# The cosine table of a rotary embedding loaded in two transfers, rows 0 to 15 and rows 16 to 127

## The chip, the core and the metric

The kernel runs on one core of a Trainium2 chip. The core has a vector engine (DVE), a scalar engine (ACT), GpSimd (POOL), a sync engine (SP) and a tensor engine (PE), which this kernel leaves idle, and sixteen DMA engines that move data between the device's memory (HBM) and the on-chip memory, whose 128 partitions are the rows of a tile. The metric is the device time of one execution in microseconds, the median of three runs.

## The reference

Rotary position embedding on x of shape (batch 8, sequence 2048, 16 heads, 64 features), float32, with tables cos and sin of shape (2048, 32):

```python
x1 = x[..., :head_dim // 2]
x2 = x[..., head_dim // 2:]
cos = cos[None, :, None, :]
sin = sin[None, :, None, :]
out1 = x1 * cos - x2 * sin
out2 = x1 * sin + x2 * cos
return np.concatenate([out1, out2], axis=-1).astype(np.float32)
```

## The kernel before

One tile is one batch element. The 2048 positions are laid over 128 partitions, J = 16 consecutive positions to a partition, so a tile is 128 x 16384 numbers: 64 KB of float32 per partition in HBM, 32 KB of float16 on the chip. The eight tiles are loaded by DMAs that POOL issues (`load`, L54) and that turn float32 into float16 on the way; DVE rotates a tile in three passes (`rotate`: the product with sin into v, L75; the product with cos in place, L81; the sum, L83); DMAs from POOL store the tile back, float16 to float32 (`store`, L62). Five buffers hold tiles, so load b + 5 waits until store b has landed.

Three loads go through SP's own DMA queue, which doesn't convert: sin (L42), the first four positions of each partition of tile 0 as float32 (`head`, JA = 4, L43, 16 KB per partition), and cos (L47, 2 KB per partition), in this order. POOL's load of tile 0 therefore brings only positions 4 to 15 (48 KB per partition in HBM).

ACT turns these into float16: it writes sin twice into sin_h, once negated (L94, L95), narrows head's first position (JF = 1, `narrow_head(0, JF)`, L89), narrows cos into cos_h (L97), then head's other three positions (L89 again). DVE rotates the first position of tile 0 by itself (128 x 1024), and POOL stores it at once as `first` (L108, `store_rows`).

Order around the start. Each engine runs its own instructions in order. The order on POOL is fixed by hand for the start (`ring`): load 0, load 1, the first store, load 2, load 3, load 4; then the stores and loads of the main loop. The first store waits for DVE's L83 on the first position, which waits for L81, which needs cos_h. The order of the other engines' instructions comes from a scheduler that starts from the order of the program and may move instructions that don't depend on each other.

The end: the last tile goes out in three parts, positions 0 to 8 (L136), 9 to 13 (L138) and, as float32 through ACT's copy `tail` (L147) and SP's queue (L148), positions 14 and 15, which wait until the first part has landed.

Of the kernel before, what the change touches and what calls it, by code (L numbers as in the profile page):

```python
# [1 line left out]

# [4 lines left out]


@with_exitstack  # L10
def kernel(
    ctx: ExitStack,
    tc: tile.TileContext,
    x: bass.AP,
    cos: bass.AP,
    sin: bass.AP,
    out: bass.AP,
):
    nc = tc.nc
    f16 = mybir.dt.float16  # L20
    f32 = mybir.dt.float32

    B, S, H, D = x.shape
    Dh = D // 2
    P = nc.NUM_PARTITIONS
    J = S // P
    NBUF = 5

    const_pool = ctx.enter_context(tc.tile_pool(name="rope_const", bufs=1))
    io_pool = ctx.enter_context(tc.tile_pool(name="rope_io", bufs=NBUF))  # L30
    tmp_pool = ctx.enter_context(tc.tile_pool(name="rope_tmp", bufs=1))

    JA = 4
    JE = 2
    JF = 1
    head = io_pool.tile([P, JA, H, D], f32, tag="xt")
    x0 = x[0].rearrange("(p j) h d -> p j (h d)", j=J)
    sin_f = const_pool.tile([P, J, Dh], f32)
    cos_f = const_pool.tile([P, J, Dh], f32)
    cos_h = const_pool.tile([P, J, Dh], f16)  # L40
    sin_h = const_pool.tile([P, J, D], f16)
    nc.sync.dma_start(out=sin_f, in_=sin.rearrange("(p j) d -> p j d", j=J))  # L42
    nc.sync.dma_start(  # L43
        out=head.rearrange("p j h d -> p (j h d)"),
        in_=x0[:, 0:JA, :].rearrange("p j f -> p (j f)"),
    )
    nc.sync.dma_start(out=cos_f, in_=cos.rearrange("(p j) d -> p j d", j=J))  # L47

    loads = []

    def load(b):
        xt = io_pool.tile([P, J, H, D], f16, tag="xt")
        j0 = JA if b == 0 else 0
        dma = nc.gpsimd.dma_start(  # L54
            out=xt[:, j0:J, :, :].rearrange("p j h d -> p (j h d)"),
            in_=x[b].rearrange("(p j) h d -> p j (h d)", j=J)[:, j0:J, :].rearrange("p j f -> p (j f)"),
        )
        loads.append(dma)
        return xt

    def store(b, xt, j0=0):
        return nc.gpsimd.dma_start(  # L62
            out=out[b].rearrange("(p j) h d -> p j (h d)", j=J)[:, j0:J, :].rearrange("p j f -> p (j f)"),
            in_=xt[:, j0:J, :, :].rearrange("p j h d -> p (j h d)"),
        )

    def rotate(xt, j0, j1):
        v = tmp_pool.tile([P, J, H, D], f16)
        n = j1 - j0
        js = slice(j0, j1)  # L70
        shape = [P, n, H, 2, Dh]
        sin_b = sin_h[:, js, :].rearrange("p j (e d) -> p j e d", e=2).unsqueeze(2).to_broadcast(shape)
        cos_b = cos_h[:, js, :].unsqueeze(2).to_broadcast([P, n, 2 * H, Dh])
        xe = xt[:, js, :, :].rearrange("p j h (e d) -> p j h e d", e=2)
        nc.vector.tensor_mul(  # L75
            out=v[:, js, :, :].rearrange("p j h (e d) -> p j h e d", e=2),
            in0=xe[:, :, :, ::-1, :],
            in1=sin_b,
        )
        xw = xt[:, js, :, :].rearrange("p j h (e d) -> p j (h e) d", d=Dh)  # L80
        nc.vector.tensor_mul(out=xw, in0=xw, in1=cos_b)  # L81
        xa = xt[:, js, :, :].rearrange("p j h d -> p (j h d)")
        nc.vector.tensor_add(out=xa, in0=xa, in1=v[:, js, :, :].rearrange("p j h d -> p (j h d)"))  # L83


    tiles = [load(0)]
    tiles.append(load(1))
    def narrow_head(j0, j1):
        nc.scalar.copy(  # L89
            out=tiles[0][:, j0:j1, :, :].rearrange("p j h d -> p (j h d)"),  # L90
            in_=head[:, j0:j1, :, :].rearrange("p j h d -> p (j h d)"),
        )

    nc.scalar.copy(out=sin_h[:, :, Dh:D], in_=sin_f)  # L94
    nc.scalar.mul(out=sin_h[:, :, 0:Dh], in_=sin_f, mul=-1.0)  # L95
    narrow_head(0, JF)
    nc.scalar.copy(out=cos_h, in_=cos_f)  # L97
    narrow_head(JF, JA)
    rotate(tiles[0], 0, JF)
    def part(b, j0, j1):  # L100
        return (
            out[b].rearrange("(p j) h d -> p j (h d)", j=J)[:, j0:j1, :].rearrange("p j f -> p (j f)"),
            tiles[b][:, j0:j1, :, :].rearrange("p j h d -> p (j h d)"),
        )

    def store_rows(b, j0, j1):
        dst, src = part(b, j0, j1)
        return nc.gpsimd.dma_start(out=dst, in_=src)  # L108

    first = store_rows(0, 0, JF)  # L110
    ring = [loads[0], loads[1], first]
    for b in range(2, NBUF):
        tiles.append(load(b))
        ring.append(loads[b])
    for a, b in zip(ring[1:], ring[:-1]):
        tc.add_manual_dep(
            a.ins,
            b.ins.name,
            mybir.DependencyInfo(mybir.DependencyClass.NoSync, mybir.DependencyReason.DATA),
            reason="order of the ring",  # L120
        )
    for b in range(B):
        rotate(tiles[b], JF if b == 0 else 0, J)
        if b < B - 1:
            st = store(b, tiles[b], JF if b == 0 else 0)
            if b == 0:
                tc.add_manual_dep(
                    st.ins,
                    first.ins.name,
                    mybir.DependencyInfo(mybir.DependencyClass.NoSync, mybir.DependencyReason.DATA),  # L130
                    reason="order of the ring",
                )
        if b + NBUF < B:
            tiles.append(load(b + NBUF))
    dst, src = part(B - 1, 0, 9)
    gate = nc.gpsimd.dma_start(out=dst, in_=src)  # L136
    dst, src = part(B - 1, 9, J - JE)
    rest = nc.gpsimd.dma_start(out=dst, in_=src)  # L138
    tc.add_manual_dep(
        rest.ins,  # L140
        gate.ins.name,
        mybir.DependencyInfo(mybir.DependencyClass.NoSync, mybir.DependencyReason.DATA),
        reason="order of the ring",
    )
    dst, src = part(B - 1, J - JE, J)
    tail = io_pool.tile([P, JE, H, D], f32, tag="xt")
    nc.scalar.copy(out=tail.rearrange("p j h d -> p (j h d)"), in_=src)  # L147
    end = nc.sync.dma_start(out=dst, in_=tail.rearrange("p j h d -> p (j h d)"))  # L148
    tc.add_manual_dep(
        end.ins,  # L150
        gate.ins.name,
        mybir.DependencyInfo(mybir.DependencyClass.Sync, mybir.DependencyReason.DATA),
        reason="the last rows go out behind this part",
    )


# [1 line left out]
_INS = ['x', 'cos', 'sin']  # L158
_OUTS = [((8, 2048, 16, 64), 'float32')]


# [23 lines left out]
```

## Time and profile before

| | |
|---|---|
| median of three runs | 316.67 us (316.46 to 317.0) |
| profiled execution, first to last instruction (span) | 314.8 us; no other time is listed for it |
| DVE busy | 209.1 us, 66% of the span |
| DMA moved | HBM read 67.63 MB, written 67.11 MB, 428 GB/s over the span |
| sin: issue to landing | 2.8 us, 256 KB |
| head: issue to landing | 16.4 us, 2048 KB |
| cos: issue to landing | 34.1 us, 256 KB |
| load 0: issue to landing | 22.0 us, 3072 KB on the chip |
| first store: issue to landing | 6.4 us, 512 KB on the chip |

Two views matter most. The chain of waits follows the last instruction back to what released it; the timeline lists instructions with start, length, engine and line, and in brackets how long the engine sat idle before and what ended that. "q0" are the packets of DMAs that POOL issued, "q1" those that SP issued. Beside these views the trace keeps a record of each DMA packet, with start, length, size and queue: one packet per row of a transfer, and for each DMA engine a 4-byte completion packet that counts up the semaphore. Landing times are those of the last of sixteen completions.

### The profile page before, as it was taken

The numbers are of one execution on the slowest core, as the hardware profiler recorded it, in microseconds if no ns is written. First come the engines' busy times: TensorE is split into PE (matmuls) and PEld (weight loads), VectorE is DVE, ScalarE is ACT, GpSimd is POOL, SyncE is SP. The second block draws the span as 40 slices with busy tenths as digits, with TensorE's granted clock in tenths as the row PEclk, the third lists the DMA queues.
The fourth block names the chain that finished last, engine by engine and source line by source line (L and its number), as shares of the span: only waits on it lengthen the run. The fifth ranks groups of instructions, "written<-read, shape, count | busy, mean of one in ns | idle before, by whom it ended". The sixth has DMA issues, their size and how long they took to land.

```text
span 314.8 us, 126 instructions
## 1 busy us (share of the span) xinstructions
DVE 209.1 (66%) x27; ACT 8.6 (3%) x7; POOL 9.9 (3%) x22
## 2 busy tenths in 40 slices
DVE  0000299999999999999999999999009993000000
ACT  3010400000000000000000000000000002000000
POOL 1000110000000000010000000200000001000000
DMA  8999999999999899999999999999999999999998
GB/s 262 287 233 212 204 267 200 200 266 200 200 200 325 375 500 400 400 333 266 200 200 208 391 400 400 458 475 266 200 266 466 400 400 516 416 400 400 433 425 341
DMA packets 3168, 102.24 MB, mean 325 GB/s; under 512 B 352, under 2 KB 352, under 8 KB 736
## 3 DMA queue, kind: packets, MB, share of 16 engines
q0 software_dynamic: 2592, 98.57, 97.4%
q1 hardware_dynamic: 576, 3.67, 3.0%
HBM read 67.63 MB, written 67.11 MB: 428 GB/s over the span
## 4 chain that ended last, share of the span: by engine, by line
DMA 39%; DVE 24%; issue 18%; ACT 2%; POOL 0%; SPq 0%; POOLq 0%; DVEq 0%
DMA out_dram<-xt 16%; DMA xt<-in_x_dram 12%; DMA cos_f<-in_cos_dram 11%; DVE xt L83 8%; DVE xt L81 8%; DVE v L75 8%; ACT xt L89 1%; ACT tail L147 1%; POOL out_dram L62 0%; ACT cos_h L97 0%; POOL xt L54 0%; SPq L43 0%; SPq L42 0%; POOLq L54 0%; DVEq L75 0%
## 5 line engine op out<-in xcount | busy, mean ns | idle before, releaser
L75 DVE TENSOR_TENSOR v<-xt,sin_h 128x16384 f16<-128x16384 f16 (+2 forms) x9 | 69.7, 7744 | 35.9 <-ACT xt L89 19.8
L81 DVE TENSOR_TENSOR xt<-xt,cos_h 128x16384 f16<-128x16384 f16 (+2 forms) x9 | 69.7, 7744 | 17.4 <-ACT cos_h L97 17.1
L83 DVE TENSOR_TENSOR xt<-xt,v 128x16384 f16<-128x16384 f16 (+2 forms) x9 | 69.7, 7744 | 0.3
L147 ACT CAST tail<-xt 128x2048 f32<-128x2048 f16 x1 | 1.9, 1898 | 223.7 <-DVE xt L83 223.7
L54 POOL DMA_DIRECT2D xt<-in_x_dram x8 | 4.4, 555 | 105.4 <-DMA out_dram<-xt 104.6
L62 POOL DMA_DIRECT2D out_dram<-xt x7 | 3.7, 535 | 71.4 <-DVE xt L83 71.4
L89 ACT CAST xt<-head 128x1024 f16<-128x1024 f32 (+1 forms) x2 | 3.8, 1896 | 12.9 <-DMA head<-in_x_dram 12.9
L136 POOL DMA_DIRECT2D out_dram<-xt x1 | 0.5, 531 | 41.5 <-DVE xt L83 41.5
L108 POOL DMA_DIRECT2D out_dram<-xt x1 | 0.5, 536 | 35.7 <-DVE xt L83 35.7
L94 ACT ACT_TABLE_LOAD x1 | 1.3, 1283 | 0.7 <-PEq L169 0.7
L97 ACT CAST cos_h<-cos_f 128x512 f16<-128x512 f32 x1 | 0.6, 617 | 17.2 <-DMA cos_f<-in_cos_dram 17.2
L94 ACT CAST sin_h<-sin_f 128x512 f16<-128x512 f32 x1 | 0.6, 617 | 1.5 <-DMA sin_f<-in_sin_dram 1.5
L95 ACT ACTIVATE sin_h<-sin_f 128x512 f16<-128x512 f32 x1 | 0.6, 624 | 0.0
L138 POOL DMA_DIRECT2D out_dram<-xt x1 | 0.5, 531 | 0.0
L169 POOL MEMSET const-float32-0.0<- 128x1 f32 x1 | 0.1, 98 | 0.2 <-issue 0.2
L169 POOL MEMSET const-bfloat16-1.0<- 128x1 bf16 x1 | 0.1, 102 | 0.0
L169 POOL MEMSET const-float32-1.0<- 128x1 f32 x1 | 0.1, 98 | 0.0
L169 POOL MEMSET const-uint8-127<- 128x1 uint8 x1 | 0.1, 98 | 0.0
## 6 DMA issues: line engine op xcount, KB each, us to landing
xt<-in_x_dram POOLq DMA_DIRECT2D x7, 4096.0 KB, 38.3
out_dram<-xt POOLq DMA_DIRECT2D x1, 7680.0 KB, 56.7
out_dram<-xt POOLq DMA_DIRECT2D x1, 4608.0 KB, 42.4
xt<-in_x_dram POOLq DMA_DIRECT2D x1, 3072.0 KB, 22.0
out_dram<-xt POOLq DMA_DIRECT2D x1, 2560.0 KB, 47.9
head<-in_x_dram SPq DMA_DIRECT2D x1, 2048.0 KB, 16.4
out_dram<-tail SPq DMA_DIRECT2D x1, 1024.0 KB, 8.4
out_dram<-xt POOLq DMA_DIRECT2D x1, 512.0 KB, 6.4
```

Of the source, the lines that this page charges most:

```text
L54: dma = nc.gpsimd.dma_start(out=xt[:, j0:J, :, :].rearrange("p j h d -> p (j h d)"), in_=x[b].rearrange("(p j) h d -> p j (h d)", j=J)[:, ...
L62: return nc.gpsimd.dma_start(out=out[b].rearrange("(p j) h d -> p j (h d)", j=J)[:, j0:J, :].rearrange("p j f -> p (j f)"), in_=xt[:, j0:J ...
L75: nc.vector.tensor_mul(out=v[:, js, :, :].rearrange("p j h (e d) -> p j h e d", e=2), in0=xe[:, :, :, ::-1, :], in1=sin_b,)
L81: nc.vector.tensor_mul(out=xw, in0=xw, in1=cos_b)
L83: nc.vector.tensor_add(out=xa, in0=xa, in1=v[:, js, :, :].rearrange("p j h d -> p (j h d)"))
L89: nc.scalar.copy(out=tiles[0][:, j0:j1, :, :].rearrange("p j h d -> p (j h d)"), in_=head[:, j0:j1, :, :].rearrange("p j h d -> p (j h d)"),)
L94: nc.scalar.copy(out=sin_h[:, :, Dh:D], in_=sin_f)
L95: nc.scalar.mul(out=sin_h[:, :, 0:Dh], in_=sin_f, mul=-1.0)
L97: nc.scalar.copy(out=cos_h, in_=cos_f)
L108: return nc.gpsimd.dma_start(out=dst, in_=src)
L136: gate = nc.gpsimd.dma_start(out=dst, in_=src)
L147: nc.scalar.copy(out=tail.rearrange("p j h d -> p (j h d)"), in_=src)
```

## The change

The DMA that SP issues for cos is replaced by two, in the same place of SP's order: rows 0 to 15 first, then rows 16 to 127. Both views are written as 128 rows of 512 contiguous floats; the bytes read and written are the same.

```diff
-    nc.sync.dma_start(out=cos_f, in_=cos.rearrange("(p j) d -> p j d", j=J))
+    K = 16
+
+    def load_table(table, source):
+        rows = source.rearrange("(p j) d -> p (j d)", j=J)
+        flat = table.rearrange("p j d -> p (j d)")
+        nc.sync.dma_start(out=flat[0:K], in_=rows[0:K])
+        nc.sync.dma_start(out=flat[K:P], in_=rows[K:P])
+
+    load_table(cos_f, cos)
```

In the built program SP has one DMA more (16 x 512 and 112 x 512 for 128 x 512). ACT's conversion of cos waits for two semaphores in place of one, and the scheduler places it behind the narrowing of head's positions 1 to 3, where it stood ahead of it. The order on DVE and POOL stays the same. Lines from L48 on move down by eight: `load` is at L62, `store` at L70, `rotate`'s three passes at L83, L89 and L91, narrow_head at L97, cos_h at L105 and the first store at L116.

## The prediction

> **What bounds the kernel now.** I read the page first: engine shares, DMA row, queues.
>
> ```profile
> DVE 209.1 (66%) x27; ACT 8.6 (3%) x7; POOL 9.9 (3%) x22
> ...
> DMA  8999999999999899999999999999999999999998
> ...
> q0 software_dynamic: 2592, 98.57, 97.4%
> q1 hardware_dynamic: 576, 3.67, 3.0%
> ```
>
> No compute engine is near full, while the two DMA queues together fill 97.4 + 3.0 = 100.4% of sixteen engines' span (packets overlap a little). The trace's packet records run from 1.79 to 313.57 us of a 314.8 us span with no hole. So the end moves only if transfers cost more engine time, or if the engines run dry somewhere; a wait elsewhere is paid only through such a hole.
>
> Next the chain of waits, its early part, because it begins with the transfer that changes:
>
> ```profile
> 1.63 34.15 DMA cos_f<-in_cos_dram
> 35.78 0.02 issue
> 35.80 0.62 ACT cos_h L97
> 36.42 2.66 ACT xt L89
> 39.08 0.02 issue
> 39.10 8.17 DVE v L75
> ```
>
> Cosine is 256 KB and takes 34 us to land. Then the timeline from there:
>
> ```profile
> 36.45 0.69 DVE L81 TENSOR_TENSOR xt<-xt,cos_h 128x1024 f16<-128x1024 f16 x1 [17.14 <-ACT cos_h L97]
> 37.18 0.69 DVE L83 TENSOR_TENSOR xt<-xt,v 128x1024 f16<-128x1024 f16 x1
> 38.16 0.54 POOL L108 DMA_DIRECT2D out_dram<-xt  x1 [35.71 <-DVE xt L83]
> 38.69 1.59 POOL L54 DMA_DIRECT2D xt<-in_x_dram  x3
> 39.10 8.16 DVE L75 TENSOR_TENSOR v<-xt,sin_h 128x15360 f16<-128x15360 f16 x1 [1.24 <-ACT xt L89]
> ```
>
> This is the place to watch: POOL's queue is in order, and the first store (L108) waits for cosine through ACT and DVE, with loads 2, 3 and 4 behind it. Until it is issued, POOL's ring holds only loads 0 and 1.
>
> **Why cosine takes 34 us.** The packet records give the turns of a DMA engine (each engine moves 8 rows of a 128-row transfer and one 4-byte completion packet; starts are those of the first engine, the others follow within 0.4 to 0.6 us). Once both queues have work, one packet of SP's queue alternates with one of POOL's: head's row 8 at 14.38, a load 0 row at 15.00, head's completion packet at 16.81, a load 0 row at 16.82, cosine row 1 at 18.62, load 0 at 18.72, row 2 at 20.53, load 0 at 20.62, row 3 at 22.43, load 0's completion packet at 22.52, row 4 at 22.53, then rows 5 to 8 at 25.02, 27.52, 30.03 and 32.53 with load 1's rows between, and cosine's completion packet at 35.04. A completion packet thus takes a turn of its own, and a turn costs a whole row of the load: 2.41 to 2.50 us here. Load 1's last two rows start at 37.45 and 39.87, its completion packet at 42.62, and the first store's rows at 42.64 with no pause; load 2 follows at 43.88.
>
> **The change, part by part.** (1) One transfer of 128 rows becomes two of 16 and 112 rows. 16 and 112 both divide by 16, so I give each engine 1 row and 7 rows: still 8 rows, but two completion packets. The work added is 16 packets of about 0.02 us, one per engine: 0.02 us. In the ring the first part's completion packet takes the turn at 20.53, each later row moves one turn down, row 8 goes at 35.04 and the second completion packet at 37.45, where load 1's seventh row now starts. Cosine lands 37.45 - 35.04 = 2.41 us later, at 38.19.
> (2) SP issues one more DMA: 0.42 us (the row of L47), done by 2.5 us, 16 us before the first turn it needs. Nothing is behind it on SP until the last rows at 305.53. Cost nothing; without that cover, 0.42.
> (3) cos_h now waits for two semaphores, and ACT's instructions stand in another order: the narrowing of head rows 1 to 3 (2.75 us) comes ahead of cos_h. It then runs at about 18.6 under the wait for cosine, and the large DVE L75 no longer waits the 1.24 us for it. DVE's long chain starts at 37.87 + 2.41 + 0.02 = 40.30 rather than 39.10.
> (4) What is late next is L108: 38.16 + 2.41 = 40.57, with loads 2 to 4 at its heels (0.53 each).
> (5) The later issues keep far ahead of the ring: the store of 63.94 has its first packet at 101.85, the load of 140.54 at 158.60, the one of 198.24 at 216.56, the store of 263.05 at 293.82. 1.2 to 2.4 us more is covered by at least 18 us. Without that cover DVE's 1.2 us would come on top.
>
> So everything hangs on one price that the trace doesn't show directly: L, the time from POOL's issue of a DMA to its first packet on an engine that is free for it. The store must be in the ring by 42.64. In the old kernel any L up to 42.64 - 38.16 = 4.48 was hidden; in the new one up to 42.64 - 40.57 = 2.07. Upper bound: load 0, the only POOL transfer issued onto an empty ring, was issued at 1.25 and its first packet ran at 5.28, which is 4.03 us. Every engine had by then run exactly four head rows of 0.62 us. If alternation is strict, load 0 wasn't there when the fourth was picked, so L lies in 4.03 - 0.62 = 3.41 to 4.03. Lower bound: SP's own sin, issued at 0.74, first packet at 1.79: 1.05 us. I take the POOL row, being the same engine, kind and path, at its middle: 3.7 us.
>
> Sum: first packet of the store at 40.57 + 3.7 = 44.27 in place of 42.64: sixteen engines idle for about 1.63 us, plus 0.02 of completion packets = +1.65. Load 2 is issued 0.53 us behind the store, whose own packets last 1.2 us, so it adds nothing. The profiled execution's span becomes 314.8 + 1.65 = 316.4. Its span is 1.9 us below the median of the runs, 316.67, which also count what lies around the first and last instruction; I add the same to the median: 318.3. L of 3.41 and 4.03 give +1.36 and +1.98, so 318.0 to 318.7; L of 1.05 gives 316.7.
>
> **The rivals.** *Not slower: the ring is refilled in time.* This needs L below 2.07. For it: the last rows (L148) were issued by SP at 305.53 and began only at 310.73, when POOL's ring had drained, although SP needs 1.05 us on free engines; so engines seem to accept several packets ahead. If that held for load 0 too, the four head rows ahead of it (4 x 0.62 = 2.48) were accepted earlier, and L is 4.03 - 2.48 = 1.55: store in the ring at 42.12, half a microsecond before it is needed, change 0.02, time 316.7. Against it: in turns 14.38 to 35.04 alternation is strict, and 1.55 leaves only 0.5 us of margin. The Trainium skill (DMA: Bandwidth & Descriptors, Specifications) gives about 1 us to the first byte for DMAs from GpSimd and 0.6 us from SP; by that the store would be in the ring by about 41.6 and the time would stay at 316.7, but SP's measured 1.05 is already above its figure, and no row here shows POOL's on idle engines.
>
> *The first part doesn't cost a turn* (its completion packet rides along with its row). Then cosine lands at 35.8 as before and the time is 316.7. Against it: head's completion packet at 16.81 had load rows on both sides.
>
> *DVE holds POOL's descriptors back.* The old store was issued in the DVE gap from 37.87 to 39.10; the new one falls under L75, 40.30 to 48.46. If nothing reached the ring before L75 ended, the store would start 5.8 us late: 322.5. Against it: the store issued at 63.94, under L75, took 0.54 us, as long as the one of 263.05 with DVE idle (0.53). The Trainium skill (SBUF — State Buffer, Who interferes with whom) says that a two-input DVE operation collides only with GpSimd's reads of SBUF, not its writes; the equal 0.54 agrees.
>
> *The parts are spread over fewer engines*, say eight rows to each: the 16-row part on two engines, which may then also hold eight rows of the other. Row 9 would go at 37.45, row 10 at 39.87, the other six without partners after 42.6, landing near 43.7, so L108 near 46.1 and its packet at 47.6 (L 1.55) to 49.8 (L 3.7): +5.0 to +7.2, about 322.8. Against it: 22 transfers have 352 small packets, 16 each.
>
> **How the numbers follow.** Dry ring, as summed: 0.46. Refilled in time: 0.38. No extra turn: 0.05. Held-back descriptors and fewer engines: 0.04 each. Something that makes it faster: 0.03; the engines have no hole to close and no work is taken out, so I know of none. A measurement of this kernel tells no less than about 0.2% (0.63 us) from no change: slower holds the dry ring and the two dear cases, 0.54; same 0.43; faster 0.03. The likeliest case's own range is 317.4 to 318.8. The range, 316.4 to 319.0, takes in both ends of L with the runs' own scatter (316.46 to 317.0) and leaves out the dear cases.
>
> **What would show it.** Right: 8 rows and two completion packets of cosine per engine, cos_h at about 38.2, ACT's long narrowing at 18.6, L108 at 40.6, large L75 at 40.3, then a hole of 1.3 to 2 us across the engines after 42.6, and every later transfer late by that. If there is no hole, L was below 2.07 and the first rival holds. If cos_h stays at 35.8, the turn was wrong; if it is beyond 40, the spread was. If L108 is on time but its rows start near 48.5, DVE held them. I'd be wrong altogether if the engines stay full and the end still moves.

## The result, and the profile after

The changed kernel takes 318.44 us (median of five runs, 318.05 to 319.24) against 316.61 us (316.46 to 317.0) for the old one beside it: ratio 1.0058, 95% interval 1.0046 to 1.0071, or 1.8 us slower. On two of the chips used for the experiments some runs, of the old kernel too, were 2 to 9 us longer, and the ratios leave out only those over 1.5% above the fastest, so the medians and the profiled spans are compared as well. The profiled execution of the changed kernel has a span of 317.5 us, 2.7 more than the old one's 314.8; the spans of its five runs go from 316.3 to 317.5.

The page of the changed kernel (DMA row, queues, and the first store's line among the DMA issues):

```profile
DMA  8999999999999999999999999999999999999995
...
q0 software_dynamic: 2592, 98.57, 96.8%
q1 hardware_dynamic: 592, 3.67, 3.0%
...
out_dram<-xt POOLq DMA_DIRECT2D x1, 512.0 KB, 4.3
```

SP's queue has 16 packets more, one completion packet for each DMA engine. The engines' row is still full except for its last slice. The first store now lands 4.3 us after its issue (6.4 before): it doesn't come to an empty ring, it comes just in time.

The timeline of the changed kernel around cosine (start, length, engine, line, operation):

```profile
17.62 3.70 ACT L97 CAST xt<-head 128x1024 f16<-128x1024 f32 x2 [13.06 <-DMA head<-in_x_dram]
...
38.32 0.62 ACT L105 CAST cos_h<-cos_f 128x512 f16<-128x512 f32 x1 [17.00 <-DMA cos_f<-in_cos_dram]
38.97 0.69 DVE L89 TENSOR_TENSOR xt<-xt,cos_h 128x1024 f16<-128x1024 f16 x1 [19.58 <-ACT cos_h L105]
39.70 0.69 DVE L91 TENSOR_TENSOR xt<-xt,v 128x1024 f16<-128x1024 f16 x1
40.42 8.16 DVE L83 TENSOR_TENSOR v<-xt,sin_h 128x15360 f16<-128x15360 f16 x1
40.68 0.54 POOL L116 DMA_DIRECT2D out_dram<-xt  x1 [38.23 <-DVE xt L91]
41.21 1.60 POOL L62 DMA_DIRECT2D xt<-in_x_dram  x3
```

Cosine is 2.5 us later (38.32 for 35.80), both narrowings of head stand together at 17.62, the first store is issued at 40.68 for 38.16, the long DVE pass starts at 40.42 for 39.10.

Where the time is lost is seen on POOL's loads, each of which waits for a store to land. Timelines of POOL, first of the old kernel, then of the changed one:

```profile
121.23 0.53 POOL L54 DMA_DIRECT2D xt<-in_x_dram  x1 [30.57 <-DMA out_dram<-xt]
140.54 0.53 POOL L54 DMA_DIRECT2D xt<-in_x_dram  x1 [18.78 <-DMA out_dram<-xt]
...
198.24 0.53 POOL L54 DMA_DIRECT2D xt<-in_x_dram  x1 [55.22 <-DMA out_dram<-xt]
```

```profile
123.93 0.53 POOL L62 DMA_DIRECT2D xt<-in_x_dram  x1 [31.95 <-DMA out_dram<-xt]
143.22 0.53 POOL L62 DMA_DIRECT2D xt<-in_x_dram  x1 [18.76 <-DMA out_dram<-xt]
...
200.91 0.54 POOL L62 DMA_DIRECT2D xt<-in_x_dram  x1 [56.10 <-DMA out_dram<-xt]
```

Load 5, the first of them, is 2.70 us late, and the next two 2.68 and 2.67: in this execution all of the loss lies ahead of store 0's landing, none behind it.

The packet records say where ahead of it. A row of loads 1 to 4 takes 2.43 us on its engine. In the changed kernel the first store's rows start at 42.34 with no pause, but load 2's first rows, from 43.59 on, take 2.47 to 3.74 us, unevenly, and the spread between the first and the last engine goes from 0.44 to 1.7 us; then, 55 us later, load 4's last rows, from 99.27 on, take 2.78 to 3.88 us on all engines. In the old kernel both places show 2.43 (only load 1's last rows are stretched there, by 0.3 us on average, which the changed kernel doesn't show). Each engine has its own rows to move, and the one that lost most sets the end: store 0's last rows start from 117.66 to 118.01 us in the old kernel and from 118.42 to 120.68 us in the changed one, so the last is 2.67 us late, as load 5 is.

### The profile page after: what moved, and what is told of

It is laid out like the page before. It is cut to its first block, busy times and chain, and to the rows that moved or that the text cites. A ratio compares the mean times of both kernels' runs of the same rounds, so it can differ in the third digit from the quotient of the medians.

```text
span 317.5 us, 129 instructions
## 1 busy us (share of the span) xinstructions
DVE 209.1 (66%) x27; ACT 8.6 (3%) x7; POOL 9.9 (3%) x22
## 4 chain that ended last, share of the span: by engine, by line
DVE 25%; DMA 23%; issue 18%; another core or an unknown queue 16%; ACT 1%; POOL 1%; SPq 0%; POOLq 0%; DVEq 0%; ACTq 0%
DMA xt<-in_x_dram 12%; DMA cos_f<-in_cos_dram 11%; DVE xt L91 8%; DVE xt L89 8%; DVE v L83 8%; ACT tail L155 1%; POOL out_dram L70 0%; POOL xt L62 0%; ACT cos_h L105 0%; SPq L52 0%; SPq L43 0%; SPq L42 0%; POOLq L62 0%; DVEq L83 0%
## 5 line engine op out<-in xcount | busy, mean ns | idle before, releaser
L83 DVE TENSOR_TENSOR v<-xt,sin_h 128x16384 f16<-128x16384 f16 (+2 forms) x9 | 69.7, 7744 | 36.2 <-ACT xt L97 18.7
L89 DVE TENSOR_TENSOR xt<-xt,cos_h 128x16384 f16<-128x16384 f16 (+2 forms) x9 | 69.7, 7744 | 19.9 <-ACT cos_h L105 19.6
L91 DVE TENSOR_TENSOR xt<-xt,v 128x16384 f16<-128x16384 f16 (+2 forms) x9 | 69.7, 7744 | 0.3
L62 POOL DMA_DIRECT2D xt<-in_x_dram x8 | 4.4, 556 | 107.6 <-DMA out_dram<-xt 106.8
L70 POOL DMA_DIRECT2D out_dram<-xt x7 | 3.7, 535 | 67.9 <-DVE xt L91 67.9
L97 ACT CAST xt<-head 128x1024 f16<-128x1024 f32 (+1 forms) x2 | 3.7, 1896 | 13.1 <-DMA head<-in_x_dram 13.1
L116 POOL DMA_DIRECT2D out_dram<-xt x1 | 0.5, 536 | 38.2 <-DVE xt L91 38.2
L105 ACT CAST cos_h<-cos_f 128x512 f16<-128x512 f32 x1 | 0.6, 617 | 17.0 <-DMA cos_f<-in_cos_dram 17.0
```

The costliest lines, as they stand in the source:

```text
L62: dma = nc.gpsimd.dma_start(out=xt[:, j0:J, :, :].rearrange("p j h d -> p (j h d)"), in_=x[b].rearrange("(p j) h d -> p j (h d)", j=J)[:, ...
L70: return nc.gpsimd.dma_start(out=out[b].rearrange("(p j) h d -> p j (h d)", j=J)[:, j0:J, :].rearrange("p j f -> p (j f)"), in_=xt[:, j0:J ...
L83: nc.vector.tensor_mul(out=v[:, js, :, :].rearrange("p j h (e d) -> p j h e d", e=2), in0=xe[:, :, :, ::-1, :], in1=sin_b,)
L97: nc.scalar.copy(out=tiles[0][:, j0:j1, :, :].rearrange("p j h d -> p (j h d)"), in_=head[:, j0:j1, :, :].rearrange("p j h d -> p (j h d)"),)
```

## The experiments

Twelve runs. The table is made from the packet records and timelines of their profiles, one profile each; "lead" is the time from POOL's issue of load 2 to the start of its first row, and "spread after" is the time between the first and the last engine behind load 2's first rows. Ratios are against the old kernel run beside each (medians 316.54, 316.74 and 316.66 us).

```
                 first store  lead of   load 2 first   load 4 last    spread   span
                 issued       load 2    rows took      rows took      after
old              38.16        5.19      2.43           2.43           0.35     314.8
store0_late      38.09        5.27      2.43           2.43           0.34     314.8
dve_late         38.13        5.26      2.43           2.43           0.47     314.9
order_only       38.15        5.03      2.43           2.43           0.31     314.6
late_by_1_3      39.46        3.73      2.43 to 3.00   2.43           0.91     315.2
store0_early     40.66        2.61      2.43 to 3.73   2.89 to 3.71   1.5      316.9
changed          40.68        2.38      2.47 to 3.74   2.78 to 3.88   1.7      317.5
again            40.70        2.41      2.62 to 3.45   2.91 to 3.92   1.2      317.1
split_old_order  40.77        2.33      2.43 to 3.11   3.11 to 3.95   1.2      317.0
late_by_2_6      40.77        2.35      2.43 to 3.45   3.19 to 4.09   1.3      317.4
three_parts      43.08        1.82      2.62 to 3.29   3.06 to 3.87   0.7      318.1
late_by_5_3      43.40        1.89      2.49 to 3.19   3.00 to 3.67   0.5      318.2
cos_first        48.37        1.83      2.54 to 3.26   2.97 to 3.63   0.7      323.1
loads_first      40.57        40        2.43           2.92 to 3.23   0.3      315.5
```

**again.** The changed kernel, unaltered.

> The changed kernel once more, unaltered, for a second profile. In the first one the sixteen engines were not empty after 42.6 us; instead the first rows of load 2 (43.6 to 47.9 us) took 2.47 to 3.74 us in place of 2.43, unevenly, and the spread of the engines grew from 0.44 to 1.7 us; a second such place came at 99.3 us. Theory 'just in time' (load 2 is issued only 2.4 us before its first packet is due, and some engines have to wait for it): the stretch at 43.6 us comes again, the slowest engine loses 1 to 1.6 us there, time 318.0 to 318.8; the place at 99 us need not come again. Rival 'chance' (stretched packets that fall anywhere, whatever the change): they come at other times, and the time scatters between 316.6 and 319.

Measured 318.73 us (318.05 to 319.26), ratio 1.0067 (1.0052 to 1.0082). Both stretched places came back, at 43.64 and 99.4 us. "Chance" falls; they belong to the kernel.

**order_only.** The old kernel with ACT's new order.

```diff
     narrow_head(0, JF)
+    narrow_head(JF, JA)
     nc.scalar.copy(out=cos_h, in_=cos_f)
-    narrow_head(JF, JA)
```

> The old kernel, cosine in one transfer, with ACT's order of the changed kernel (head's rows 1 to 3 narrowed ahead of cos_h). The long DVE pass then starts right behind the short ones, near 37.9 us, and the first store and loads 2 to 4 are issued under it, near 38.2 us, with no delay. 'Just in time': 316.6, within 0.3. Rival 'DVE cover' (POOL's descriptors come slowly while the long DVE pass runs): about 318, with the stretched packets near 42 to 45 us. 'Chance': anything between 316.6 and 319.

Measured 316.64 us, ratio 1.0018 (0.9998 to 1.0038). Its timeline:

```profile
37.89 8.16 DVE L75 TENSOR_TENSOR v<-xt,sin_h 128x15360 f16<-128x15360 f16 x1
38.15 0.54 POOL L108 DMA_DIRECT2D out_dram<-xt  x1 [35.69 <-DVE xt L83]
38.68 1.59 POOL L54 DMA_DIRECT2D xt<-in_x_dram  x3
```

The issues fall under the long DVE pass, as in the changed kernel, and the packets stay at 2.43 us in the profile: the scheduler's move on ACT is not what costs. But eight of its ten runs lay at 316.34 to 316.94 and two at 318.80 and 318.96, while the old kernel's thirteen beside it lay at 316.46 to 316.73. Neither of the two was profiled, so whether the DVE pass now and then pushes a lead of 5.0 us over the edge is open.

**split_old_order.** The changed kernel with ACT's old order, held by a dependency.

```diff
-    nc.scalar.copy(out=cos_h, in_=cos_f)
-    narrow_head(JF, JA)
+    convert = nc.scalar.copy(out=cos_h, in_=cos_f)
+    rest_of_head = narrow_head(JF, JA)
+    tc.add_manual_dep(
+        rest_of_head.ins,
+        convert.ins.name,
...
```

> The changed kernel, cosine in two transfers, with ACT's old order (cos_h ahead of the narrowing of head's rows 1 to 3). The first store is issued near 40.6 us as in the changed kernel, but DVE stands idle for 1.24 us from 40.3 us, as it did in the old one. 'Just in time': 318.0 to 318.8, as the changed kernel. 'DVE cover': 316.6 to 317.

Measured 318.98 us (318.62 to 319.5), ratio 1.0077 (1.0062 to 1.0092). Its timeline:

```profile
40.77 0.54 POOL L122 DMA_DIRECT2D out_dram<-xt  x1 [38.31 <-DVE xt L91]
41.30 1.59 POOL L62 DMA_DIRECT2D xt<-in_x_dram  x3
41.71 8.16 DVE L83 TENSOR_TENSOR v<-xt,sin_h 128x15360 f16<-128x15360 f16 x1 [1.24 <-ACT xt L97]
```

DVE is idle until 41.71, while the store goes out and load 2 follows it, and the loss is all there. "DVE cover" falls from this side.

**late_by_2_6, late_by_1_3, late_by_5_3.** One cosine transfer, the old kernel's queues, and cos_h written five, three and nine times in place of once. The edit of the first; the others have `range(3)` and `range(9)`:

```diff
-    nc.scalar.copy(out=cos_h, in_=cos_f)
     narrow_head(JF, JA)
+    for _ in range(5):
+        nc.scalar.copy(out=cos_h, in_=cos_f)
```

> The old kernel with one cosine transfer and ACT's order of the changed one, and cos_h written five times over instead of once, so that it is ready about 4 x 0.65 = 2.6 us later; the DMA queues and their turns are those of the old kernel. 'Just in time': 318 to 319, with load 2's first packets stretched, since only the lateness of the issues counts. Rival 'the added packets' (the second completion packet itself upsets the engines' step): 316.6.

> The old kernel with ACT's order of the changed one and cos_h written three times over: about 2 x 0.65 = 1.3 us late. 'Late issue' with a threshold: the first store goes out near 39.5 us and load 2 near 40.0, 3.6 us before its first packet is due. Either clean (316.6) in most runs, or both places are there (318 to 319); a middle value of the median, 317.2 to 317.8, would speak for a cost that grows with lateness and against a threshold.

> The same with cos_h written nine times over: about 8 x 0.65 = 5.2 us late. The first store goes out near 43.4 us, after load 1's last packet at 42.3, so the engines must run empty: with the 1.7 us or less from issue to first packet that the changed kernel showed, from 42.4 to 44.5 or 45, a hole of 2 to 2.7 us. 'Late issue' with a hole alone: 318.7 to 319.4. If the stretched packets come on top: 320.5 to 322.

The first is the central one: 318.98 us (318.31 to 319.15), ratio 1.0072 (1.0057 to 1.0087), with both stretched places, and no second transfer in it. Its timeline:

```profile
35.81 3.21 ACT L99 CAST cos_h<-cos_f 128x512 f16<-128x512 f32 x5 [14.57 <-DMA cos_f<-in_cos_dram]
...
40.77 0.54 POOL L109 DMA_DIRECT2D out_dram<-xt  x1 [38.32 <-DVE xt L83]
41.30 1.59 POOL L54 DMA_DIRECT2D xt<-in_x_dram  x3
```

Cosine lands as early as in the old kernel; cos_h, and with it the first store and the loads behind it, is as late as in the changed one. This lateness alone makes the whole effect.

At 1.3 us the ratio can't be told from one (0.9996, 0.9971 to 1.0020): nine of the ten runs lay at 316.50 to 317.25 and one at 325.21, the median, 317.07, is 0.3 us above the old kernel's 316.74, and the span is 315.2. Two engines show the first place, none the second. So most of the cost sets in between leads of 3.7 and 2.6 us; whether there is a threshold, or the first place grows with the lateness, one profile at each lead doesn't settle.

At 5.2 us it is 320.07 us (319.97 to 320.59), ratio 1.0100 (1.0068 to 1.0132), and the ring does run dry. Windows of that kernel (stretch, length, busy time of DVE, ACT, POOL, clock, DMA share, GB/s; a packet counts where it starts):

```profile
42.00:43.00 1.00, 0.97 (x2) 0.00 (x0) 0.00 (x0) 1.00 0.02 0
43.00:44.00 1.00, 0.97 (x2) 0.00 (x0) 0.60 (x2) 1.00 0.00 0
44.00:45.00 1.00, 1.00 (x1) 0.00 (x0) 1.00 (x3) 1.00 0.65 229
```

No row starts from 42 to 44 us. The store was issued at 43.40 and its first row ran at 44.50: 1.10 us. That is the price that the prediction had to bound. The span nearly adds up: a hole of 2.1 us, 0.5 us (means over the engines) at load 2's first rows and 0.9 at load 4's last, less the 0.3 which the old kernel loses at load 1's last rows and this one doesn't: 3.2 for a measured 3.4. The run lies between the two ranges expected: the stretch does come on top of the hole, and costs less than I had allowed for it.

**loads_first.** The changed kernel with loads 2 to 4 ahead of the first store on POOL.

```diff
-    first = store_rows(0, 0, JF)
-    ring = [loads[0], loads[1], first]
     for b in range(2, NBUF):
         tiles.append(load(b))
-        ring.append(loads[b])
+    first = store_rows(0, 0, JF)
+    ring = loads[0:NBUF] + [first]
```

> The changed kernel, cosine in two transfers, but POOL asks for loads 2, 3 and 4 ahead of the first store, so that none of them waits for cosine. Cosine and the first store are as late as in the changed kernel. Theory 'late issue' (what costs is that loads 2 to 4 stand behind the first store on POOL and reach the ring late): no stretched packets near 43.6 us nor near 99 us, engines' spread stays under 0.6 us, time 316.4 to 316.9. Rival 'split' (the second transfer, or the later DVE chain, upsets the engines in itself): 318 to 319 as the changed kernel.

Measured 317.38 us against 316.74, ratio 1.0017 (1.0003 to 1.0031), span 315.5. POOL's timeline:

```profile
1.25 2.26 POOL L62 DMA_DIRECT2D xt<-in_x_dram  x4 [0.80 <-PEq L187]
21.50 0.54 POOL L62 DMA_DIRECT2D xt<-in_x_dram  x1 [17.99 <-ACT xt L97]
40.57 0.54 POOL L116 DMA_DIRECT2D out_dram<-xt  x1 [18.54 <-DVE xt L91]
```

Loads 2 and 3 go out at the start, load 4 at 21.50, when head, whose buffer it takes, has been narrowed. Cosine and the long DVE pass are as late as in the changed kernel, but the first place and the spread are gone, and the loss falls from 1.8 us to 0.6. So the first place needs the late issue. The second doesn't need late loads: load 4's last rows, which now precede the first store's small rows, still take 0.5 to 0.8 us more, and some rows before them up to 0.2. The expected 316.4 to 316.9 was missed by half a microsecond.

**dve_late and store0_late.** The old kernel with spare DVE products between tile 0's long passes, to see whether the second place comes from store 0, which is issued 1.3 us later in the changed kernel: four of 0.7 us in dve_late (the scheduler put two of them ahead of store 0), two of 1.75 us in store0_late (shown).

```diff
+    spare = const_pool.tile([P, 3, J * D], f16)
...
+        for _ in range(extra):
...
+            again = nc.vector.tensor_mul(out=spare, in0=wide, in1=wide)
```

> The old kernel with four spare DVE products of 0.7 us laid between the long passes of tiles 0 and 1, so that DVE's chain and the stores behind it are 1.4 to 2.8 us later, while the first store and loads 2 to 4 are issued as in the old kernel. In the changed kernel the second place of stretched packets is the last row of load 4, near 99.3 us. Theory 'the engines' uneven step' (that place is a consequence of the spread which the first place leaves): none here, 316.4 to 316.9. Rival 'late stores' (stores 0 and 1 issued 1.3 us later make it): stretched packets at 99 us, time 317 to 318.

> The old kernel with two spare DVE products laid between the long passes of tile 0, so that store 0 (the long one) is issued 2.5 us or more later, while the first store and loads 2 to 4 go out as in the old kernel. So far the second place of stretched packets (the last row of load 4) came in every kernel in which store 0 was issued 2.2 us or more after load 3's first row had started, and in none in which it was 1.6 us or less. Theory 'store 0 late against the ring': the stretch at 99.4 us appears, 0.4 to 1.2 us on all engines, nothing at 43.6 us, time 317.2 to 317.9. Rival 'it follows from the first place': no stretch, 316.4 to 316.9.

Both are the old kernel again: ratios 1.0002 (0.9966 to 1.0038) and 1.0002 (0.9974 to 1.0030), spans 314.9 and 314.8. In dve_late store 0 is only 0.9 us later (64.87 for 63.94), less than the 1.3 in question, so the test is store0_late. POOL there:

```profile
38.09 0.54 POOL L120 DMA_DIRECT2D out_dram<-xt  x1 [35.64 <-DVE xt L95]
38.62 1.60 POOL L54 DMA_DIRECT2D xt<-in_x_dram  x3
66.96 0.54 POOL L62 DMA_DIRECT2D out_dram<-xt  x1 [26.75 <-DVE xt L95]
```

Store 0 goes out 3.0 us later than in the old kernel, and load 4's rows stay at 2.43 us. The theory that I had formed by then, store 0 late against the ring, falls.

**store0_early.** The other side of it; the kernel leaves out the sum for positions 1 to 15 of tile 0.

```diff
-        nc.vector.tensor_add(out=xa, in0=xa, in1=v[:, js, :, :].rearrange("p j h d -> p (j h d)"))
+        if n != J - JF:
+            nc.vector.tensor_add(out=xa, in0=xa, in1=v[:, js, :, :].rearrange("p j h d -> p (j h d)"))
```

> The changed kernel without DVE's sum (the third pass) for positions 1 to 15 of tile 0, which is left out of the computation, so that store 0 is issued 8.2 us earlier; the first store and loads 2 to 4 are as late as in the changed kernel. 'Store 0 late against the ring': the stretch at 43.6 us stays (slowest engine 1 to 1.5 us), the one at 99.3 us goes, time 317.4 to 318.1. Rival 'it follows from the first place': both stay, 318.0 to 319.2.

Measured 318.62 us, ratio 1.0052 (1.0031 to 1.0074). Its POOL timeline:

```profile
40.66 0.54 POOL L117 DMA_DIRECT2D out_dram<-xt  x1 [38.21 <-DVE xt L92]
41.18 1.59 POOL L62 DMA_DIRECT2D xt<-in_x_dram  x3
57.04 0.54 POOL L70 DMA_DIRECT2D out_dram<-xt  x1 [14.26 <-DVE xt L89]
```

Store 0 is 8 us earlier than in the changed kernel and both places stay. So the second one doesn't come from store 0. That it follows from the late issue of loads 2 to 4, whose last row it is, isn't shown: loads_first has it without.

**cos_first.** Both cosine transfers ahead of head.

```diff
-    nc.sync.dma_start(
-        out=head.rearrange("p j h d -> p (j h d)"),
-        in_=x0[:, 0:JA, :].rearrange("p j f -> p (j f)"),
-    )
...
     load_table(cos_f, cos)
+    nc.sync.dma_start(
+        out=head.rearrange("p j h d -> p (j h d)"),
+        in_=x0[:, 0:JA, :].rearrange("p j f -> p (j f)"),
+    )
```

> Cosine in two transfers as in the changed kernel, but asked for ahead of head, so that both parts have landed before POOL's first packets and no turn is lost. cos_h is ready near 5 us, the first store goes out near 21 us, DVE's long chain starts near 23 us, when load 0 has landed. 'Late issue': no stretch that isn't in the old kernel, time 316.3 to 316.9, so that the second transfer costs nothing by itself. Rival 'split': 317.5 or more.

A plain miss: 325.2 us (324.93 to 325.74), ratio 1.0260 (1.0226 to 1.0293). Its timeline:

```profile
20.55 0.62 ACT L105 CAST cos_h<-cos_f 128x512 f16<-128x512 f32 x1 [15.77 <-DMA cos_f<-in_cos_dram]
44.85 3.70 ACT L97 CAST xt<-head 128x1024 f16<-128x1024 f32 x2 [23.69 <-DMA head<-in_x_dram]
...
48.37 0.54 POOL L116 DMA_DIRECT2D out_dram<-xt  x1 [45.92 <-DVE xt L91]
```

I had thought that cosine's rows would pass before POOL's first packets. Those of the first part did; those of the second alternated with POOL's from about 5 us on, and head, whose first four rows had gone through unopposed in the old order, then lost a turn for each of its eight rows and landed at 44.8. An engine stood empty for 6.2 us on average (all sixteen together from 44.55 to 49.48). The first row of the store again ran 1.11 us after its issue (49.48). The question it was to answer, whether a second transfer without a late first store costs anything, it leaves open; late_by_2_6 shows from the other side that the lateness costs as much without one.

**three_parts.** Cosine in transfers of 16, 16 and 96 rows.

```diff
-        nc.sync.dma_start(out=flat[K:P], in_=rows[K:P])
+        nc.sync.dma_start(out=flat[K:2 * K], in_=rows[K:2 * K])
+        nc.sync.dma_start(out=flat[2 * K:P], in_=rows[2 * K:P])
```

> Cosine in three transfers, of 16, 16 and 96 rows: one completion packet more, one turn of 2.41 us more. cos_h near 40.7 us, first store near 43.1, its first packet 1.0 to 1.3 us later, a hole of about 2 us from 42.3 us. Time 319.4 to 320.3. Rival (a turn is lost only once, not for each transfer): 318.0 to 319.0.

Four runs: 319.84 and 319.94, as expected, and 322.65 and 323.73, above it; ratio 1.0160 (1.0097 to 1.0223), so how much slower it is stays unclear. The profiled one is that of 319.84, span 318.1.

```profile
40.72 0.62 ACT L106 CAST cos_h<-cos_f 128x512 f16<-128x512 f32 x1 [19.49 <-DMA cos_f<-in_cos_dram]
...
43.08 0.54 POOL L117 DMA_DIRECT2D out_dram<-xt  x1 [40.63 <-DVE xt L92]
```

cos_h comes at 35.80, 38.32 and 40.72 us with one, two and three transfers: 2.5 and 2.4 us for each. All engines are empty from 42.71 on, and the store's first row, at 44.19, came 1.11 us after the issue.

## Why the prediction was right in its number and wrong in its reason

*The turn.* Right. The records show the first part's completion packet at 20.57, eight rows and two completion packets per engine, the last from 37.50 on; 38.19 was predicted for the landing, and ACT started at 38.32.

*ACT's order, L108 and DVE.* Right: the narrowing of head's positions 1 to 3, the second of the pair that starts at 17.62, begins at 18.57, the store is issued at 40.68 and the long pass starts at 40.42; 18.6, 40.57 and 40.30 were predicted. The ample cover of the later issues is borne out for store 0: issued 3 us later (store0_late) or 8 us earlier (store0_early), it changes nothing.

*The price L.* This is the first step that failed: "I take the POOL row, being the same engine, kind and path, at its middle: 3.7 us". Where the engines really stood empty, it was 1.10, 1.11 and 1.11 us (late_by_5_3, cos_first, three_parts). The Trainium skill (DMA: Bandwidth & Descriptors, Specifications) gives about 1 us for the first byte of a GpSimd DMA, and these three runs agree with it. Load 0's 4.03 us contained head's four rows, as the first rival argued: in cos_first, where head comes later, load 0's first row ran at 2.80, 1.56 us after its issue at 1.24. The rival's 1.55 was the better estimate.

*The hole after 42.6 us.* Wrong: there is none in the changed kernel; the store's rows run at 42.34. What was predicted to be a common idle time of 1.63 us on sixteen engines is, in the profiled execution, a loss of about 1.0 us on average and 2.7 us on the slowest engine (starts of store 0's last rows), in two places, inside packets that take longer. That the sum, 1.65, comes close to the measured 1.8 is luck.

*The rival "refilled in time".* It had the right L and the right first packet, and the wrong time (316.7). It was priced at nothing because I asked only whether the store would be in the ring when the engines needed it. This is the second step that failed: "Load 2 is issued 0.53 us behind the store, whose own packets last 1.2 us, so it adds nothing". Load 2's first rows lost 0.4 us on average and up to 1.3 us. The runs order themselves by the lead of load 2: at 5.0 us and more its first rows take 2.43 us, at 3.7 a few are longer, at 2.6 and less up to 1.3 us longer. The store and load 2 were late together in every run that shows the place, so the table can't tell the lead of one from the lead of the other.

*Descriptors held back by DVE; fewer engines.* Neither: the store's rows ran 1.7 us after its issue, under the long pass, and each engine had its eight rows.

What isn't settled is what happens inside a stretched row, and why load 4's last row, 55 us on, is stretched too. It isn't the engines' spread, which is 0.5 us in late_by_5_3 with 0.9 us of stretch, nor store 0, nor the second transfer, nor ACT's order, nor late loads alone, since loads_first has it. In the table it goes with the issue of the first store: the nine profiles with it have that store at 40.57 us or later, the five without at 39.46 or earlier. No run moves that store with the loads left where they are. That something of POOL's loads still has to be written when the engines reach them would fit the first place, but POOL's instructions for the three loads end at 42.81 us in the changed kernel, 0.8 us ahead of the first stretched row; what follows them isn't in the trace.

## What to carry to other kernels

When a second DMA queue alternates packet by packet with a queue of large rows, every transfer in it costs one turn more than its rows, here 2.4 us, and so does everything placed ahead of it: an order that favours one table delays another. Ask of the transfers behind a late issue not only whether they reach the ring before it is empty, but with how much lead; here 2.6 us were too little and 3.7 nearly enough, though the first packet takes only 1.1. And a price read from a row in which another queue had work ahead is an upper bound, not a value.

## What the runs showed of the hardware that was not expected

A row of a load took up to 1.3 us longer than its 2.43 when it was asked for 2.6 us ahead or less, and the last row of the last load issued with it did the same, up to 1.66 us, in all eight profiles with such a late issue (and up to 0.8 us in loads_first, which had none). Once the DMA engines are out of step they stay so while they have work: in the changed kernel the spread of 1.7 us at 48 us is still 1.7 at 80 us, and 2.3 us from 120 to 290 us. Running empty brought them together: in cos_first it is 2.1 us at load 1's last rows and 0.1 us at the first store's, behind the hole.
